# Holes of four partitions in both the loads and the scatters of five groups, and a reset instead of a drain, in a rank-and-scatter kernel

## The chip, the cores and the metric

The kernel runs on one core of a Trainium2 chip. The metric is the device time of one execution in microseconds (us). All executions quoted here count as fast ones. The kernel before takes 775.2 us (median of 4 executions beside the changed kernel, 775.0 to 775.73).

## The reference

Each row of 2,560 floats of `x` goes to the row of the output that its score's rank names, batch by batch:

```python
B, N, D = 8, 2048, 2560
order = np.argsort(scores, axis=1)
ranks = np.argsort(order, axis=1)
out[b_idx, ranks, :] = x          # 168 MB read, 168 MB written
```

The arithmetic is small (DVE counts, for each score, how many others of its batch are smaller). The work is to move 168 MB in and 168 MB out.

## The kernel before

A batch is cut into eight groups of 256 rows; in a group each of the 128 partitions holds two neighbouring rows of `x` (20,480 bytes). 58 groups go through eight buffers: Pool issues a load, and later two indirect scatters of 128 rows of 10,240 bytes. The first group of batches 0 to 5 takes another way: SP and ACT copy its rows one by one from DRAM to DRAM (the "row copies").

A transfer (DMA) is split over 16 DMA engines into packets: in the trace each of Pool's 204 loads and scatters shows as 128 packets, one per partition, and 16 that count up a semaphore; each row copy as 16 packets of 640 bytes and 16 of 4. A "hole" is four partitions of a group that its scatters leave out; their eight rows go by row copies instead. "The engine of 48-51" (or of 44-47) is short for the DMA engine that a hole at these partitions relieves. The trace names no engines, but it shows the relief: in the kernel before, the two scatters of group (5,4), with a hole at 48-51, take the part of one engine from 0.1 us behind the other late one to 2.3 us ahead of it. "Landing" is the moment at which a part of a transfer is reported done.

```python
DIRECT = range(6)            # batches whose group 0 goes by row copies
NBUF, LAG = 8, 4
THIN = {**{(b, 4): 48 for b in range(1, B)}, (7, 5): 44}   # the holes: (batch, group): first partition
HALVED = range(32)           # loads issued in two halves of 10,240 bytes per partition
# ... for a group in THIN, N is added to the ranks of four partitions: out of bounds, so not scattered
nc.gpsimd.indirect_dma_start(
    out=out_flat,
    out_offset=bass.IndirectOffsetOnAxis(ap=rank_i[:, col:col + 1], axis=0),
    in_=xb[k % NBUF][:, j * D:(j + 1) * D], in_offset=None, element_offset=b * N * D,
    **(dict(bounds_check=N - 1, oob_is_err=False) if (b, g) in THIN else {}),
).then_inc(s_scat[k % NBUF][j], 16)
# ... and the eight rows of a hole are row copies too (thin_rows)

for k, (b, g) in enumerate(BULK):                 # Pool's loop
    if k >= LAG and k + NBUF - LAG < len(BULK):
        scatters_done(pl, k - LAG)                # buffer free
        load_ahead(k + NBUF - LAG)
    pl.wait(*loaded[k])
    pl.after(dve, t_bulk[b, g])                   # ranks of this group
    for j in range(GROUPS[g][1]):
        scatter(k, j)
nc.gpsimd.drain()
for k in range(max(0, len(BULK) - NBUF), len(BULK)):
    scatters_done(sp, k)
```

## Time and profile before

| what | number | where |
|---|---|---|
| time | 775.2 us | executions |
| span of the profiled execution | 772.8 us | page |
| DVE, the busiest compute engine | 400.7 us busy | page, part 1 |
| moved by DMA | 320.15 MB, mean 414 GB/s | page, part 2 |
| last of the 16 parts of the last scatter lands | 770.56 us | semaphore records |
| from there to the end of the span | 2.24 us | the same |

The prediction shows the DMA rows. Two more views of the kernel before: First the page's part of the costliest groups: line, engine, operation, output and input, count; then busy us and mean ns; then the engine's idle time ahead of them and what ended most of it.

```profile
L424 POOL DMA_INDIRECT out_dram<-x,rank_i x116 | 113.4, 977 | 139.6 <-issue 35.0
L126 POOL DMA_DIRECT2D x<-in_x_dram x88 | 49.4, 565 | 436.9 <-DMA out_dram<-x,rank_i 418.5
```

Pool's own work is 113 + 49 us of 773; it stands idle 437 us ahead of its loads. It has room for dearer issues. Second, the page's list of DMA issues: output and input, queue, count and KB each:

```profile
x<-in_x_dram POOLq DMA_DIRECT2D x62, 1280.0 KB
x<-in_x_dram POOLq DMA_DIRECT2D x26, 2560.0 KB
out_dram<-in_x_dram ACTq DMA_DIRECT2D x800, 10.0 KB
out_dram<-in_x_dram SPq DMA_DIRECT2D x800, 10.0 KB
```

62 half loads and 26 whole ones by Pool, and 800 row copies on each of ACT and SP: 128 for each of six batches, and 32 for the holes.

### The profile page before, as it was taken

The numbers are of one execution on the slowest core, as the hardware profiler recorded it, in microseconds if no ns is written. First come the engines' busy times: TensorE is split into PE (matmuls) and PEld (weight loads), VectorE is DVE, ScalarE is ACT, GpSimd is POOL, SyncE is SP. The second block draws the span as 40 slices with busy tenths as digits, with TensorE's granted clock in tenths as the row PEclk, the third lists the DMA queues.
The fourth block names the chain that finished last, engine by engine and source line by source line (L and its number), as shares of the span: only waits on it lengthen the run. The fifth ranks groups of instructions, "written<-read, shape, count | busy, mean of one in ns | idle before, by whom it ended". The sixth has DMA issues, their size and how long they took to land.

```text
span 772.8 us, 8228 instructions
## 1 busy us (share of the span) xinstructions
PE 36.2 (5%) x172; PEld 30.4 (4%) x172; DVE 400.7 (52%) x828; ACT 0.0 (0%) x1; POOL 164.6 (21%) x213
## 2 busy tenths in 40 slices
PE   4000020020020020030000000000000000000000
PEld 3000010010010010030000000000000000000000
DVE  5999979979979979979999500000000000000000
ACT  0000000000000000000000000000000000000000
POOL 4114223222213131312112121212121212112100
PEclk8555555555555555565555555555555555555555
DMA  8999999999999999999999999999999999999996
GB/s 358 418 418 420 418 418 418 418 417 418 418 420 417 420 417 417 419 417 419 416 421 421 422 416 426 416 427 417 422 417 424 417 426 415 424 418 424 419 414 283
DMA packets 80898, 320.15 MB, mean 414 GB/s; under 512 B 28968, under 2 KB 54568, under 8 KB 54568
## 3 DMA queue, kind: packets, MB, share of 16 engines
q0 software_dynamic: 29376, 300.82, 91.7%
q1 hardware_dynamic: 25904, 10.93, 5.2%
q10 hardware_dynamic: 25600, 8.24, 4.3%
q14 instruction: 17, 0.14, 0.0%
q8 instruction: 1, 0.02, 0.0%
HBM read 168.49 MB, written 168.43 MB: 436 GB/s over the span
## 4 chain that ended last, share of the span: by engine, by line
DMA 63%; DVE 13%; another core or an unknown queue 9%; POOL 6%; issue 4%; PE 1%; POOLq 0%; SPq 0%
DMA out_dram<-x,rank_i 57%; DVE trash L239 12%; DMA x<-in_x_dram 6%; POOL out_dram L424 4%; POOL x L126 2%; PE ps_all L196 0%; DVE s_all L341 0%; DMA s_in<-in_scores_dram 0%; PE ps_col L175 0%; POOLq L448 0%; DVE rank_i L277 0%; DVE rank L271 0%; DVE rank L265 0%; PE ps_row L300 0%
## 5 line engine op out<-in xcount | busy, mean ns | idle before, releaser
L239 DVE TENSOR_SCALAR_CACHE_REDUCE trash<-s_all,s_col 128x1792 bf16<-128x1792 f32 (+7 forms) x240 | 315.2, 1348 | 4.6
L424 POOL DMA_INDIRECT out_dram<-x,rank_i x116 | 113.4, 977 | 139.6 <-issue 35.0
L126 POOL DMA_DIRECT2D x<-in_x_dram x88 | 49.4, 565 | 436.9 <-DMA out_dram<-x,rank_i 418.5
L239 DVE SCALAR_TENSOR_TENSOR trash<-s_all,s_col,mask 128x256 bf16<-128x256 f32 x128 | 61.6, 482 | 0.0
L196 PE MATMUL ps_all<-ident,s_col 128*128 128x128 f32 x128 | 28.1, 411 | 3.2 <-DVE s_all L341 2.8
L300 PE MATMUL ps_row<-ident,rank 128*1 128x128 f32 x28 | 8.3, 398 | 393.6 <-DVE rank_i L286 386.4
L196 PEld LDWEIGHTS ps_all<-ident,s_col 128*128 128x128 f32 x128 | 26.5, 222 | 4.2 <-DVE s_all L341 3.2
L341 DVE COPY s_all<-ps_all 128x512 f32<-128x512 f32 x32 | 20.2, 685 | 1.5 <-PE ps_all L196 1.1
L239 DVE DVE_READ_ACCUMULATOR trash<-s_all,s_col 128x1 f32 x240 | 19.9, 83 | 0.0
L300 PEld LDWEIGHTS ps_row<-ident,rank 128*1 128x1 f32 x28 | 2.0, 97 | 397.9 <-DVE rank_i L286 389.5
L311 DVE TENSOR_SCALAR thin_i<-ps_row 1x8 int32<-1x8 f32 x8 | 1.2, 154 | 19.0 <-PE ps_row L300 19.0
L239 DVE DVE_READ_ACCUMULATOR trash<-s_all,s_col,mask 128x1 f32 x128 | 10.7, 83 | 0.0
L326 DVE TENSOR_SCALAR rows_i<-ps_row 1x256 int32<-1x256 f32 x6 | 2.5, 412 | 4.1 <-PE ps_row L300 4.1
L183 DVE COPY s_col<-ps_col 128x128 f32<-128x128 f32 x1 | 0.3, 293 | 4.7 <-PE ps_col L175 4.7
L175 PE MATMUL ps_col<-ident,s_in 8*128 8x8 f32 x16 | 2.1, 262 | 3.9 <-DMA s_in<-in_scores_dram 3.9
L286 DVE TENSOR_SCALAR rank_i<-rank,hole 128x2 int32<-128x2 f32 x8 | 2.1, 262 | 0.3
L175 PEld LDWEIGHTS ps_col<-ident,s_in 8*128 8x128 f32 x16 | 2.0, 211 | 3.9 <-DMA s_in<-in_scores_dram 3.9
L277 DVE CAST rank_i<-rank 128x16 int32<-128x16 f32 (+3 forms) x11 | 1.9, 173 | 0.4
L271 DVE TENSOR_TENSOR rank<-rank,acc 128x16 f32<-128x16 f32 (+3 forms) x11 | 1.9, 171 | 0.4
L265 DVE TENSOR_TENSOR rank<-acc,acc 128x16 f32<-128x16 f32 (+3 forms) x11 | 1.9, 170 | 0.4
L156 POOL TENSOR_SCALAR_AFFINE_SELECT mask<-mask 128x256 f32<-128x256 f32 x2 | 0.8, 398 | 0.0
L168 DVE MEMSET acc<- 128x128 f32 x1 | 0.2, 165 | 1.1 <-SPq L102 1.1
(10 smaller groups left out, 1.8 us busy)
## 6 DMA issues: line engine op xcount, KB each, us to landing
x<-in_x_dram POOLq DMA_DIRECT2D x62, 1280.0 KB
x<-in_x_dram POOLq DMA_DIRECT2D x26, 2560.0 KB
out_dram<-in_x_dram ACTq DMA_DIRECT2D x800, 10.0 KB
out_dram<-in_x_dram SPq DMA_DIRECT2D x800, 10.0 KB
x<-in_x_dram SPq DMA_DIRECT2D x2, 1280.0 KB, 9.1
out_dram<-x,rank_i POOLq DMA_INDIRECT x116, 49.0
s_in<-in_scores_dram SPq DMA_DIRECT2D x1, 64.0 KB
```

The source lines that it names most:

```text
L126: line.eng.dma_start(out=xb[k % NBUF][:, part], in_=rows[:, part]).then_inc(sem, 16)
L175: nc.tensor.transpose(out=ps_col[:, B * c:B * (c + 1)], in_=s_in[:, r + j:r + m * P:m], identity=ident[:B, :B],)
L196: nc.tensor.transpose(out=ps_all[:, P * c:P * (c + 1)], in_=s_col[:, c, b:b + 1].to_broadcast([P, P]), identity=ident[:],)
L239: do(out=trash[i][:, :P * (hi_c - lo_c)], in0=s_all[:, P * lo_c:P * hi_c], accum_out=acc[i][:, col:col + 1], **how,)
L265: nc.vector.tensor_tensor(out=rank[:, cols], in0=acc[0][:, cols], in1=acc[1][:, cols], op=OP.add)
L271: nc.vector.tensor_tensor(out=rank[:, cols], in0=rank[:, cols], in1=acc[2][:, cols], op=OP.add)
L277: nc.vector.tensor_copy(out=rank_i[:, cols], in_=rank[:, cols])
L286: nc.vector.tensor_scalar(out=rank_i[:, cols], in0=rank[:, cols], scalar1=hole[:, i:i + 1], scalar2=None, op0=OP.add,)
L300: nc.tensor.transpose(out=ps_row[:1, P * j:P * (j + 1)], in_=rank[:, col:col + 1], identity=ident[:],)
L326: nc.vector.tensor_scalar(out=rows_i[b][:].rearrange("o (p j) -> o p j", p=P), in0=ps_row[:1, :WIDE].rearrange("o (j p) -> o p j", p=P), s ...
L341: nc.vector.tensor_copy(out=s_all[:, 512 * q:512 * (q + 1)], in_=ps_all[:, 512 * q:512 * (q + 1)],)
L424: nc.gpsimd.indirect_dma_start(out=out_flat, out_offset=bass.IndirectOffsetOnAxis(ap=rank_i[:, col:col + 1], axis=0), in_=xb[k % NBUF][:, ...
```

## The change

Its intent: a hole in the load as well as in the scatter should relieve the DMA engine of those partitions twice (by the packets' measured times, the four holes at 48-51 by 24.0 us, where seven in the scatters alone gave 21.0), so that five holes do the work of eight; fewer rows then go by row copies; and the end no longer waits for a drain. To leave a hole in a load, the load becomes a gather: an indirect load that takes its rows from a list (`thin_row`), in which the rows of the hole are out of bounds. The kernel before ends Pool's work with `drain()`, the changed one with `dma_reset()`: begun after the last landing, the drain took 2.60 us (run 5) and the reset 0.30 us.

```diff
-    THIN = {**{(b, 4): 48 for b in range(1, B)}, (7, 5): 44}
+    THIN = {**{(b, 4): 48 for b in range(1, B, 2)}, (7, 5): 44}
+    THIN_LOADS = [k for k in THIN if k[0]]
-    HALVED = range(32)
+    HALVED = range(34)
 ...
+            if (b, g) in THIN_LOADS:
+                i = HOLES.index(THIN[b, g])
+                line.after(dve, t_thin[0])
+                nc.gpsimd.indirect_dma_start(
+                    out=xb[k % NBUF][:, :m * D], out_offset=None,
+                    in_=x.rearrange("b (q j) d -> (b q) (j d)", j=m),
+                    in_offset=bass.IndirectOffsetOnAxis(ap=thin_row[:, i:i + 1], axis=0),
+                    element_offset=(b * N + r) * D, bounds_check=P - 1, oob_is_err=False,
+                ).then_inc(sem, 16)
 ...   # thin_row: two DVE operations after batch 0; partition number, plus N in the hole
-        nc.gpsimd.drain()
         for k in range(max(0, len(BULK) - NBUF), len(BULK)):
-            scatters_done(sp, k)
+            scatters_done(pl, k)
+        nc.gpsimd.dma_reset()
```

(`FLAT = ()` and the function `copies` only reshape the row-copy loop; they change none of its instructions.)

More of the change, by code (lines that the diff above doesn't have):

```diff
@@ L63 @@
     G = 16
-    THIN = {**{(b, 4): 48 for b in range(1, B)}, (7, 5): 44}
+    FLAT = ()
+    THIN = {**{(b, 4): 48 for b in range(1, B, 2)}, (7, 5): 44}
     HOLES = sorted(set(THIN.values()))
-    HALVED = range(32)
+    THIN_LOADS = [k for k in THIN if k[0]]
+    HALVED = range(34)
     STEPS = [(0, 1), (1, 2), (2, 4), (4, 8)]
@@ L90 @@
     hole = pool.tile([P, len(HOLES)], F32, name="hole")
+    below = pool.tile([P, 1], F32, name="below")
+    thin_row = pool.tile([P, len(HOLES)], I32, name="thin_row")
     thin_i = {k: pool.tile([1, 4 * MMAX], I32, name=f"thin_i{k[0]}_{k[1]}") for k in THIN}
@@ L118 @@
         n_load = [0] * NBUF
+        t_thin = []
         def load(line, k, sem):
@@ L122, in load @@
             r, m = GROUPS[g]
+            if (b, g) in THIN_LOADS:
+                i = HOLES.index(THIN[b, g])
+                line.after(dve, t_thin[0])
+                nc.gpsimd.indirect_dma_start(
+                    out=xb[k % NBUF][:, :m * D],
+                    out_offset=None,
+                    in_=x.rearrange("b (q j) d -> (b q) (j d)", j=m),
+                    in_offset=bass.IndirectOffsetOnAxis(ap=thin_row[:, i:i + 1], axis=0),
+                    element_offset=(b * N + r) * D,
+                    bounds_check=P - 1,
+                    oob_is_err=False,
+                ).then_inc(sem, 16)
+                n_load[k % NBUF] += 1
+                return
             rows = x[b, r:r + P * m, :].rearrange("(p j) d -> p (j d)", j=m)
@@ L334, in rows_to_bytes, with thin_rows_of_loads @@
             )
+        def thin_rows_of_loads():
+            dve.did(
+                nc.vector.tensor_reduce(
+                    out=below[:], in_=mask[:, MMAX, :], axis=mybir.AxisListType.X, op=OP.add
+                )
+            )
+            dve.after(dve, dve.n)
+            t_thin.append(
+                dve.did(
+                    nc.vector.tensor_scalar(
+                        out=thin_row[:],
+                        in0=hole[:],
+                        scalar1=below[:],
+                        scalar2=None,
+                        op0=OP.add,
+                    )
+                )
+            )
         for b in range(B):
@@ L358 @@
                         thin_to_bytes(b, g)
+            if b == 0:
+                thin_rows_of_loads()
         n_rows = {sp: 0, act: 0}
@@ L391, with copies @@
                 half = WIDE // 2
-                with line.eng.Fori(0, half // G) as q:
+                def copies(q):
+                    first = b * N + GROUPS[0][0] + half * h
                     _, at = nc.values_load_multi_w_load_instructions(
@@ L402 @@
                     for i in range(G):
-                        row = b * N + GROUPS[0][0] + half * h + i
                         line.eng.dma_start(
                             out=out_bytes[bass.ds(at[i], ROW)],
-                            in_=x_bytes[bass.ds(q * (G * ROW) + row * ROW, ROW)],
+                            in_=x_bytes[bass.ds(q * (G * ROW) + (first + i) * ROW, ROW)],
                         ).then_inc(s_rows[line], 16)
+                if b in FLAT:
+                    for q in range(half // G):
+                        copies(q)
+                else:
+                    with line.eng.Fori(0, half // G) as q:
+                        copies(q)
                 n_rows[line] += half
```

## The prediction

> **What bounds the kernel now.** I looked first at the page's rows of busy tenths. Every compute engine is light: DVE, the busiest, works 400.7 of 772.8 us and ends shortly after 400. The row that is full from start to end is DMA's.
>
> ```profile
> DMA  8999999999999999999999999999999999999996
> GB/s 358 418 418 420 418 418 418 418 417 418 418 420 417 420 417 417 419 417 419 416 421 421 422 416 426 416 427 417 422 417 424 417 426 415 424 418 424 419 414 283
> ...
> q0 software_dynamic: 29376, 300.82, 91.7%
> q1 hardware_dynamic: 25904, 10.93, 5.2%
> q10 hardware_dynamic: 25600, 8.24, 4.3%
> ```
>
> The tenths stay at 9 in slices 2 to 39; only the first slice (start) and the last (283 GB/s against some 418) are lower. The three queues' shares add up to over 100% of 16 engines' time. So I read the packet records one by one: from 2 us on, a packet starts as the one before it on its DMA engine ends, and in the whole run I find only some 20 holes of 0.3 us. On its engine a packet of 10,240 bytes takes 381 ns, one of 20,480 bytes 757, one of 640 bytes 28 and one of 4 bytes (a semaphore) 6. The time is therefore each DMA engine's own sum of packets, and the end is that of the slowest engine of the 16. What sets it is which packets that engine has, not a wait.
>
> The view of the waits seems to say otherwise:
>
> ```profile
> POOL x L126 <- DMA out_dram<-x,rank_i: 418.5, 45, 11.2
> POOL out_dram L424 <- issue: 35.0, 108, 1.5
> POOL out_dram L424 <- DMA x<-in_x_dram: 34.6, 4, 10.8
> POOL out_dram L424 <- DVE rank_i L286: 25.7, 1, 25.7
> ```
>
> Pool waits 418.5 us for scatters before it may reload a buffer. But while it waits [...] (a scatter lands 49.0 us after its issue), so these waits starve nothing, and neither does the one of 25.7 us for DVE's ranks: the load issued before it still landed 7 us after it ended.
>
> Then I looked at the end. The semaphore records give the landing of each of the 16 parts of a DMA. For the last scatter twelve parts land 4.6 to 3.6 us before the last one, two at 3.0 and 2.5 us before it, one 1.2 us before it, and the last at 770.56 us. Two engines are thus late, by some 4 and 3 us against the twelve. For SP's queue the waits show what follows:
>
> ```profile
> SPq L28 <- DMA out_dram<-x,rank_i: 33.1, 8, 12.5
> SPq L392 <- DVE rows_i L326: 15.6, 1, 15.6
> SPq L102 <- POOLq L102: 0.9, 1, 0.9
> ```
>
> SP has its last scatter at 770.58 us and is then held 0.9 us by Pool. The record of the drain explains it:
>
> ```profile
> engine op xcount: duration ns min/median/max, first and last start us, forms
> L448 POOLq DRAIN  x1: 32437/32437/32437, 739.5 to 739.5; - x1
> ```
>
> It ends at 739.48 + 32.44 = 771.92 us, 1.36 us after the last landing. The closing barrier follows, and the span ends at 772.8: 2.24 us lie between the last landing and the end.
>
> [...] The trace names no engines[...]: in the scatters of group (5,4), whose hole is 48-51, the engine that trailed the other late one by 0.1 us is ahead of it by 2.3 us afterwards; 8 packets of 381 ns are 3.05 us.[...]
>
> What a skipped row costs can be counted: 88 loads and 116 scatters of Pool are 204 DMAs, and 204 * (128 + 16) = 29376, the packets of q0, although 64 rows were skipped; in the records 64 packets of 4 bytes are there beyond the 204 * 16 semaphores. A skipped row is a 4-byte packet of some 6 ns.
>
> Why the late engines are late: the 10,240-byte packets that took more than 386 ns come, after 430 us, in runs of some 14, some 430 ns apart, every 13 us. That is one engine, in its two scatters (then the only transfers with that size), at some 20 to 27 ns extra a packet. The holes at 48-51 pay for that; the change pays more with fewer holes.
>
> **The change part by part.**
>
> (1) Row copies. 8 holes of 8 rows were 64 rows; 5 holes are 40. 24 row copies fall away, each 28 + 6 = 34 ns on every engine: -0.82 us on all 16.
>
> (2) Engine of 48-51. Before: 7 groups, 56 scatter packets skipped, 56 * (381 - 6) = 21.0 us. After: 4 groups, 32 scatter packets, 12.0 us, and now also 4 * 4 load packets of 20,480 bytes, 16 * (757 - 6) = 12.0 us; together 24.0. It gains 3.0 us. It processes 24 more scatter packets, at some 20 ns extra each: 0.5 us back. Net -2.5.
>
> (3) Engine of 44-47. Before: 8 * 375 ns = 3.0 us. After: the same and 4 * 751 ns = 3.0 more. Net -3.0.
>
> (4) Halved loads. Groups (1,4) and (3,4), number 10 and 24 in the order, were halved and are now gathers; the limit of 34 halves numbers 32 and 33 instead. So 62 half loads remain, and 21 whole loads and 5 gathers stand for 26 whole ones: no net packets.
>
> (5) Pool's issue. An indirect issue takes 977 ns on Pool and a direct one 565; five gathers, two of which replace two issues each, cost about a microsecond of an engine that sits idle before its loads for 437 us. Nothing. The wait for DVE's row list comes at load 10, where the ranks of batch 0 have been waited for already by scatter 3. Two more small DVE operations (some 0.4 us) delay batch 1 by less than the 7 us of slack seen above. Nothing.
>
> (6) The end. The drain goes; Pool waits for the last scatters itself and then resets. The wait would end some 0.03 us after the landing, as SP's did. If the reset is as short as the other drains of Pool at the end (34 to 72 ns), Pool reaches the barrier some 0.15 us after the landing rather than 1.40, and 1.2 us are gained; since nothing shows the reset's cost, I take 1.1.
>
> Sum at the end of the DMA. The last packets of the engines lie at 770.1 and 769.0 (the late two), 767.7 and 767.2 (the two between) and 765.6 to 766.6 (twelve). I cannot tell which of the late two is which. After: 770.1 - 0.8 - 2.5 or 3.0 = 766.3 to 766.8; 769.0 becomes 765.2 to 765.7; the two between, which no hole touches, 766.9 and 766.4; the twelve 764.8 to 765.8. So the last engine is now an untouched one at 766.9, and the DMA ends 3.2 us sooner. With (6): 3.2 + 1.1 = 4.3 us, 775.31 - 4.3 = **771.0 us**, 0.6% less.
>
> **The rivals.** First, nothing but the end: the gathers might be dealt to the engines by another rule than loads, or a skipped load row might still move. For it: no gather is in the trace of before.[...] The engines of the holes would then be relieved by less than before (12 instead of 21 us) and the first would end some 9 us later, less 0.8: with the end's gain, about 782 us. Second, balance turned over: an engine that lags up to 6 us in the batches without hole could let buffers come free later.[...] If it does, 1 to 2 us of the gain go: 772 to 773. Third, the reset costs as much as the drain or more, since it takes the place of the drain on the path: then only the 3.2 us remain, or less, 772 to 773. Fourth, the load's own extra cost also goes with the skipped packets, or the two between shift too: 770.
>
> **Range and chances.** The sum of 4.3 has parts of different certainty: 0.8 and the packets' arithmetic are firm, the floor by the untouched engines is read from the trace; the reset is open by about a microsecond. 769.6 to 773.0 should hold it 8 times in 10. 2% is 15.5 us, out of reach on the fast side: faster 0.01, within 2% 0.97, slower 0.02 (the first rival and worse).
>
> **What would show it.** Bytes of q0 300.82 - 0.41 + 0.25 = 300.66 MB in 29376 packets as before; 25648 packets on q1 and 25088 on q10. The rows of issues: 62 half loads, 21 whole, 5 indirect loads. The sixteen parts of the last scatter should land within some 2.5 us instead of 4.6, the last near 767.4 us, and the span should end about 1.1 us after it, with no drain of 32 us. If the spread stays at 4 us or more, steps (2) and (3) are wrong; if the span ends 2 us or more after the last landing, step (6) is; if DMA's tenths fall below 9 in the middle, the second rival holds.

A last landing 3.2 us sooner and 1.1 us of the end come to 4.3 us, and 775.31 - 4.3 = 771.0 us. Terms (2) and (3) put the four partitions of a hole on one engine, and 48-51 and 44-47 on two different ones. What the traces show of it: in the kernel before, after 430 us, 12 to 15 slow packets (10,240 bytes in over 389 ns) stand together in the two scatters of a group, and only 7, 5 and 5 in the holed groups (4,4), (5,4) and (6,4). In the changed kernel two parts land late, by 6.5 and 5.4 us at 688 us against the median of the first twelve; after the load of (7,4), with its hole at 48-51, one of the two is down to 3.9 us (694 us), and after that of (7,5), with its hole at 44-47, the other to 3.0 and then 2.6 (708 and 721 us). Against the first rival: a scatter is indirect too, and its hole did relieve an engine, by 2.4 us in group (5,4). Against the second, and for the harmless waits, stands that a scatter lands 49.0 us after its issue, while the longest wait of Pool for a buffer is 11.2 us. The last row copies landed at 764.1 us (SP) and 762.1 us (ACT).

## The result, and the profile after

The changed kernel took 771.38 us (median of 4, 771.06 to 771.9) beside 775.2 us before: 3.8 us less. The ratio is 0.995, with an interval of 0.9933 to 0.9967. All ratios here are the mean time of one kernel's fast runs over that of the other's of the same rounds, so not quite the ratio of the quoted medians. Predicted were 771.0 us and a range of 769.6 to 773.0: right. (The two profiled executions took 774.87 and 771.55 us, 3.3 us apart, with spans of 772.8 and 769.8; the 0.4 us by which the spans differ less lie outside them, and the traces do not show what they are.)

The page after, rows of busy tenths, rates and queues (packets, MB, share of 16 engines):

```profile
DMA  8999999999999999999999999999999999999997
GB/s 356 420 419 418 418 421 417 417 419 419 418 417 417 416 419 417 419 419 418 417 418 418 425 417 423 417 422 419 422 417 423 419 420 422 419 425 416 426 411 332
...
q0 software_dynamic: 29376, 300.66, 92.0%
q1 hardware_dynamic: 25648, 10.85, 5.2%
q10 hardware_dynamic: 25088, 8.08, 4.2%
```

The bytes and packets of q0 and the packets of q1 and q10 are the predicted ones to the digit. DMA is full to the end as before; the last slice moves 332 instead of 283 GB/s, which fits the better balance. Pool's waits after:

```profile
POOL x L149 <- DMA out_dram<-x,rank_i: 391.3, 43, 11.1
...
POOL x L135 <- DMA out_dram<-x,rank_i: 40.3, 4, 10.3
...
POOL out_dram L476 <- DVE thin_row L369: 19.3, 1, 19.3
```

391.3 + 40.3 = 431.6 us of waits for a buffer stand for 418.5 before; four of them now come ahead of a gather (L135). The 19.3 us for `thin_row` is no new wait: before, the same 19.3 us stood under another DVE line, and the tie now falls on the last DVE instruction of that time. The gathers among the costliest groups, and the queue's issues:

```profile
L135 POOL DMA_INDIRECT x<-in_x_dram,thin_row x5 | 5.2, 1031 | 43.9 <-DMA out_dram<-x,rank_i 40.3
```

```profile
x<-in_x_dram POOLq DMA_DIRECT2D x62, 1280.0 KB
x<-in_x_dram POOLq DMA_DIRECT2D x21, 2560.0 KB
out_dram<-in_x_dram SPq DMA_DIRECT2D x792, 10.0 KB
out_dram<-in_x_dram ACTq DMA_DIRECT2D x784, 10.0 KB
...
x<-in_x_dram,thin_row POOLq DMA_INDIRECT x5
```

A gather costs Pool 1,031 ns, 466 more than a direct load's 565, on an engine with 430 us to spare. Row copies fell from 1,600 to 1,576.

The end, in the waits of SP's queue and in the record of the reset:

```profile
SPq L109 <- DMA out_dram<-in_x_dram: 27.7, 1, 27.7
...
SPq L109 <- POOLq L109: 11.1, 1, 11.1
```

```profile
L503 POOLq DRAIN  x1: 296/296/296, 768.7 to 768.7; - x1
```

SP has no scatter to wait for any more: it sees its last row copy land and waits 11.1 us for Pool, which sees the last scatter at 768.57 us, resets in 0.30 us (the reset is recorded as a drain) and closes. The span ends 1.28 us after the last landing, before 2.24 us. Of the span's 3.0 us (772.8 - 769.8), 2.0 are a sooner last landing (770.56 to 768.57) and 1.0 is the shorter end. The 16 parts of the last scatter lie within 3.6 us, before 4.6.

One measure is used from here on. The **lag** of a DMA engine is how much later its part of a scatter lands than the median of the first twelve of the 16 parts. In the last scatter of the kernel before the two largest lags are 4.2 and 2.9 us, in the changed one 2.8 and 1.8.

### The profile page after: what moved, and what is told of

The parts are those of the page before. It is cut to its first block, busy times and chain, and to the rows that moved or that the text cites. A ratio compares the mean times of both kernels' runs of the same rounds, so it can differ in the third digit from the quotient of the medians.

```text
span 769.8 us, 8160 instructions
## 1 busy us (share of the span) xinstructions
PE 33.4 (4%) x166; PEld 29.2 (4%) x166; DVE 400.1 (52%) x824; ACT 0.0 (0%) x1; POOL 167.1 (22%) x213
## 4 chain that ended last, share of the span: by engine, by line
DMA 63%; DVE 13%; another core or an unknown queue 10%; POOL 6%; issue 4%; PE 1%; POOLq 0%; SPq 0%
DMA out_dram<-x,rank_i 57%; DVE trash L262 12%; DMA x<-in_x_dram 6%; POOL out_dram L476 4%; POOL x L149 2%; DVE s_all L384 0%; POOL x L135 0%; PE ps_all L219 0%; DMA s_in<-in_scores_dram 0%; PE ps_col L198 0%; DVE rank_i L300 0%; DVE rank L294 0%; DVE rank L288 0%; PE ps_row L323 0%
## 5 line engine op out<-in xcount | busy, mean ns | idle before, releaser
L149 POOL DMA_DIRECT2D x<-in_x_dram x83 | 46.7, 564 | 393.3 <-DMA out_dram<-x,rank_i 391.3
L323 PE MATMUL ps_row<-ident,rank 128*1 128x128 f32 x22 | 5.9, 365 | 388.7 <-DVE rank_i L309 281.5
L135 POOL DMA_INDIRECT x<-in_x_dram,thin_row x5 | 5.2, 1031 | 43.9 <-DMA out_dram<-x,rank_i 40.3
```

The source lines that it names most:

```text
L135: nc.gpsimd.indirect_dma_start(out=xb[k % NBUF][:, :m * D], out_offset=None, in_=x.rearrange("b (q j) d -> (b q) (j d)", j=m), in_offset=b ...
L149: line.eng.dma_start(out=xb[k % NBUF][:, part], in_=rows[:, part]).then_inc(sem, 16)
L323: nc.tensor.transpose(out=ps_row[:1, P * j:P * (j + 1)], in_=rank[:, col:col + 1], identity=ident[:],)
```

## The experiments

Theory: each DMA engine has a fixed sum of packets; the one of partitions 48-51 is far later than the others, and holes take packets from it; reset against drain is worth 1 us. The main rivals: the gathers relieve nothing and only the 24 row copies count; the late engine is held or bounded by the buffers; the end gives nothing. Three sessions: the first four runs shared one chip and its runs of the kernel before (775.1 us, 11 executions), the last eight another (774.95 us, 9 to 10). All outputs were correct.

### 1. The end alone

The kernel before with the lines of the end alone changed:

```diff
-        nc.gpsimd.drain()
         for k in range(max(0, len(BULK) - NBUF), len(BULK)):
-            scatters_done(sp, k)
+            scatters_done(pl, k)
+        nc.gpsimd.dma_reset()
```

> The kernel before with the new end alone (Pool waits for the last scatters, then resets; no drain). Theory: in the trace the part after the last landing falls from 2.24 us to about 1.28 us, as in the changed kernel, and nothing else moves: 775.2 - 1.0 = 774.2 us. Rival: the old drain's tail is mostly time in which the trace's last landing is not the last write, so the reset only moves the wait elsewhere: 775.0 to 775.4 us.

Measured: 774.94 us (773.96 to 777.32), ratio 1.000 (0.9987 to 1.0012). A miss for the theory: nothing gained. The trace says why. Its waits of SP's queue:

```profile
SPq L102 <- DMA out_dram<-in_x_dram: 27.0, 1, 27.0
...
SPq L102 <- ACTq L102: 0.2, 1, 0.2
```

No line has SP wait for Pool: SP waits for ACT. The last landing of all is a row copy of ACT, at 772.13 us, after the last scatter at 771.56. In the kernel before the row copies had ended at 764 us. Nothing of the row copies was edited. When they end is not fixed from execution to execution (SP's at 757.5 us in the changed kernel's first trace and at 764.6 in its second, run 9). The last scatter too landed 1.0 us later than in the kernel before (771.56 against 770.56), which alone would have used up the gain: 771.56 + 1.28 = 772.84, where the span before was 772.8. So this run does not show what the end is worth. Runs 11 and 12 below test it.

### 2. The change without its end

The changed kernel with the old four lines of the end.

> The changed kernel with the old end (drain, SP waits). Theory: the two parts add up: 771.4 + 1.0 = 772.4 us, with the last landing near 768.6 us as in the changed kernel. Rival (the ends interact with the holes): 771.4 or 773 and more.

Measured: 771.6 us (770.92 to 772.06), ratio 0.9952 (0.9939 to 0.9965). In time it is 0.2 us from the changed kernel (another session). In the trace the last scatter lands at 767.19 us and the drain ends at 768.51, 1.32 us later, as before (1.36). But a row copy of SP lands only at 768.96: here too a row copy is last, and the drain is hidden behind it. The expectation, 772.4 us, was 0.8 too high: the last scatter landed 1.4 us sooner than the 768.6 that it assumed. In time, nearly all of the gain of the change came without its end; the two medians are of two sessions, so 0.2 us between them is no measurement of the end.

### 3. Holes in the scatters alone

```diff
-    THIN_LOADS = [k for k in THIN if k[0]]
+    THIN_LOADS = []
```

(and the two DVE operations for `thin_row` left out)

> The changed kernel with its five holes in the scatters alone; the loads of these groups are direct and whole rows. Theory: the engine of 48-51 has 16 load packets of 757 ns more, 12.0 us, that of 44-47 3.0 us more. If the engine of 48-51 is the last one of the changed kernel (last part at 768.57 us) the last landing comes at 780.6 us, if it is the second (767.58) at 779.6: time 782.4 to 783.4 us, with one part landing alone some 12 us after the others. Rival: the gathers relieve little, the gain was the 24 fewer row copies: 771 to 774 us.

Measured: 780.37 us (780.21 to 780.41), ratio 1.0067. The rival falls: without the holes in the loads the five holes are worse than the old eight. One part lands alone, with a lag of 11.1 us. The row of DMA shows what a single late engine looks like, a last slice of which the others fill only the first third:

```profile
DMA  8999999999999999999999999999999999999993
```

The expectation was 2 to 3 us too high: the 16 load packets gave less than 12.0 us.

### 4. No holes at all

```diff
-    THIN = {**{(b, 4): 48 for b in range(1, B, 2)}, (7, 5): 44}
-    HOLES = sorted(set(THIN.values()))
+    THIN = {}
+    HOLES = [44, 48]        # only so that the unused tile has columns
```

> No holes, no thin row copies, new end: shows each engine's own lateness. Theory: the engine of 48-51 loses its relief of 24.0 us (and processes 32 more scatter packets at some 20 ns extra, 0.6 us), that of 44-47 6.0 us, all 16 gain 40 row copies of 34 ns, 1.4 us. Last landing at 767.6 or 768.6 + 24.6 - 1.4 = 790.8 to 791.8 us, time 793.6 to 794.6 us, one part some 18 us after the second, the second some 5 to 6 us after the third. Rival (lateness is not fixed work of an engine but bounded by the buffers, so that a late engine holds up the others and the spread stays near 6 us): the DMA tenths fall below 9 in the middle and the time lies below 790 us with a spread of 6 to 10 us.

Measured: 789.8 us (789.71 to 790.29), ratio 1.019. The lateness is seen naked:

```profile
DMA  8999999999999999999999999999999999999980
GB/s 359 418 418 420 418 418 418 419 418 419 417 417 417 419 419 419 418 419 415 420 417 420 425 416 423 419 421 419 426 416 424 417 425 418 422 422 423 423 349 24
```

In the last slice one engine of 16 works (24 of some 420 GB/s). In the last scatter its lag is 21.9 us; the second engine's is 3.5, the next two have 0.9, the others under 0.3. The expected time, 793.6 to 794.6 us, was some 4 us too high: the holes had been counted at their full size. DMA stays at 9 until the others run out, so the buffers do not hold them up: the rival falls here too (the time is below 790 us as it said, but the lag is 21.9 us and not 6 to 10). The lag grows until some 710 us (4 us at 150, 10 at 290, 15 at 400, 18 at 510, 22 at 670, 23.4 at 708 us) and then no more.

Now the holes can be weighed by the lag of this engine:

| kernel | packets skipped on it | their time by the prediction's arithmetic | lag at the end | lag taken away |
|---|---|---|---|---|
| no_holes | 0 | 0 | 21.9 us | |
| scatter_holes | 32 of 10,240 bytes | 12.0 us | 11.1 | 10.8 |
| before | 56 of 10,240 | 21.0 | 4.2 | 17.7 |
| changed | 32 of 10,240, 16 of 20,480 | 24.0 | 2.8 (1.7 in a second trace) | 19.1 (20.2) |

(For the last two it is assumed that the last engine is the same one; if it is another, this one was relieved of more. Each lag in the table is of one trace. Four traces have the eight holes of before: before, end_only, end_rows and rows_only, with largest lags of 3.8 to 5.3 us and a mean of 4.3. Four have the changed kernel's holes: its own two, old_end and wait_drain, with 1.6 to 2.8 and a mean of 2.0.) Holes give 80 to 90% of what the packets alone would. Where the rest goes is partly seen: in the kernel before, slow packets beside the holed scatters of groups (4,4) to (7,4) carry 200 to 320 ns more than usual (at 453.2, 454.9, 545.4, 547.1, 650.7, 652.4, 749.1 and 751.2 us). In the changed kernel the other holed engine's lag falls in one holed scatter from 2.56 to 1.35 us: 1.2, not the 1.5 of four packets. A transfer with a hole thus gives some 0.3 us back. In the first 400 us no such packets stand out, so this is not the whole account, and why they are slow is not shown.

### 5. A drain after the waits

The changed kernel with `drain()` in place of `dma_reset()`; Pool still waits for the scatters first.

> The changed kernel with a plain drain in place of the reset; Pool still waits for its last scatters first. Tells the waits from the reset. Theory A (the drain [...]is slow by itself): the drain, begun at the last landing, still takes over 0.6 us where the reset took 0.30, and the tail after the last landing is 1.6 to 2.3 us. Theory B (the drain is short once all has landed): under 0.3 us, tail 1.3 us or less. The time is 771.2 to 771.8 us either way, since two earlier runs showed that the end is worth 0.2 us of time or less when a row copy can be the last transfer.

Measured: 772.84 us (772.53 to 773.38), ratio 0.997 (0.9957 to 0.9984). In the trace the drain begins when all has landed and takes

```profile
L503 POOLq DRAIN  x1: 2602/2602/2602, 767.8 to 767.8; - x1
```

2.60 us against 0.30 for the reset. Theory A holds in that the drain is slow with nothing left in flight; the tail is longer than it said (3.59 us, not 1.6 to 2.3). In the kernel before the drain began at 739.5 us and only 1.36 us of it came after the last landing; that it did the rest beside the transfers is an inference. The expected time, 771.2 to 771.8, was missed: here the scatters are last (767.69 us, row copies 764.7), so the tail counts in full. Against the changed kernel on the same chip (run 9, 772.06 us) it is 0.8 us slower.

### 6 and 7. One more hole on either engine

```diff
+    (6, 4): 48   added to THIN, in the scatters alone     # more_48
+    (6, 5): 44   added to THIN, in the scatters alone     # more_44
```

> The changed kernel with one more hole at 48-51, in the scatters of group (6,4) alone; 8 more row copies. Theory: the last part in the changed kernel is the engine of 48-51, 2.8 us behind the median of the twelve; eight packets fewer take 3.0 us from it, less 0.3 us for each holed transfer; 8 row copies add 0.3 us to all. Its lag falls to 0.2 to 0.8 us, the spread of the last scatter to some 2.5 us, the next engine sets the end at about 767.8 us, and the time falls 0.5 to 1.0 us, to 770.4 to 770.9. Rival (another engine is the last one): the time rises by the 0.3 us.

> The changed kernel with one more hole at 44-47, in the scatters of group (6,5) alone. Theory: the engine of 44-47 is already among the twelve at the end, so nothing is gained and the 8 row copies cost 0.3 us: 771.4 to 771.9. Rival (it is the last one): 770.4 to 770.9 us. Seen in time, its lag of 5.4 us falls by some 2.6 us at the scatters of (6,5), near 660 us, and not by 3.0, if a holed transfer gives 0.2 us back.

Measured: more_48 772.56 us (771.79 to 772.69), more_44 772.08 us (770.83 to 774.45); ratios 0.9964 and 0.9968. For more_48 the largest lag is 1.8 us, the next 1.2, and the last scatter lands at 767.54 us, near the expected 767.8. But the changed kernel's own second trace, on the same chip, has 1.7 us and 767.35 without the extra hole (run 9), so a gain from it is not shown. The time was missed: a row copy of SP lands at 769.13 us, 1.6 us after the last scatter, and closes the kernel. For more_44 the lag of the engine with the hole at 44-47 falls as expected (5.3 us at 654 us, 2.9 at 677, of which not all readings can be kept apart), and there is no gain (772.08 us, a little above the expected 771.4 to 771.9); its executions scatter over 3.6 us, and row copies (767.91 us) and scatters (767.74) end together.

### 8. Gathers without holes

The offset that put the hole's rows out of bounds is multiplied by zero, so that the gathers leave nothing out:

```diff
-    in0=hole[:], scalar1=below[:], scalar2=None, op0=OP.add,
+    in0=hole[:], scalar1=0.0, scalar2=below[:], op0=OP.mult, op1=OP.add,
```

> The changed kernel whose five gathers fetch all 128 rows; the scatters keep their holes. Against scatter_holes (780.4 us) it shows what a gather costs as such. Theory: nothing, 780.2 to 780.8 us, one part 11 us behind the others. Rival (gathers are dealt to the engines differently, or are slower): over 781.5 us, or a spread that is not that of one late engine.

Measured: 780.42 us (779.97 to 781.53), ratio 1.0071; largest lag 11.2 us. Against scatter_holes, 780.37 and 11.1: a gather as such costs nothing here. The holes in the loads are worth what lies between this and the changed kernel: 8.4 us on the same chip (772.06, run 9), 9.0 against the first session's 771.4.

### 9. The changed kernel again

> The changed kernel once more, as the yardstick on the chip of the next three: 771.1 to 771.9 us, 3.8 us under the kernel before.

Measured: 772.06 us, just above the expected range, six executions from 770.34 to 775.39, ratio 0.9965 (0.9946 to 0.9984). The profiled one (770.34) has its last landing at 767.35 us, a spread of 3.0 us and a largest lag of 1.7; the end after it is again 1.28 us. On this chip the change is worth 2.9 us (774.95 to 772.06), not 3.8. The median is 0.7 us above the first session's and one execution of six is 3.3 us above the median. The slow executions have no trace, so what they lost cannot be read.

### 10, 11 and 12. Row copies sooner

Each of these has `HALVED = range(38)`; for more_48 it stood at 34, for end_only and for the kernel before at 32.

> more_48 with 38 instead of 34 loads halved. In more_48 the row copies of SP ended last (769.1 us, 1.6 us after the last scatter). Theory: [...] the row copies end near 755 us or before, the scatters near 767.7, the tail is 1.3 us, and the time is 770.4 to 771.0, the fastest of all. Rival (the row copies' pace is set by the issue of SP and ACT[...]): they still end within 5 us of the scatters, and the time stays at 772 to 773.

> end_only with 38 instead of 32 loads halved. In end_only the row copies ended last (772.1 us) and the end gained only 0.2 us. Theory: with the row copies 20 us sooner the end shows its worth: tail 1.28 us, 774.0 to 774.4 us and a narrower spread of the runs than end_only's 3.4 us. Rival (the reset itself makes the next execution's transfers end a microsecond later): 774.8 to 775.4 us, the runs as scattered as before.

> The kernel before with 38 instead of 32 loads halved, nothing else: the control of end_rows. Theory: 48 more packets on each engine at some 5 ns more, 0.2 us; the scatters were last already, so 775.2 to 775.5 us, and end_rows lies 0.9 to 1.2 us under it. Rival: end_rows and this agree within 0.4 us.

Measured: rows_only 774.88 us (774.66 to 775.23), end_rows 773.77 us (773.06 to 774.04), more_48_rows 771.55 us (771.38 to 775.38); ratios to the kernel before 0.9995, 0.9981 and 0.9964. The first two lie 0.2 to 0.3 us below their expected ranges, the third 0.55 above: in its trace a row copy is last again (767.9 us, the last scatter 767.6).

end_rows and rows_only differ in the end alone, and in both traces the row copies end early (at 756 and 762 us at the latest). The end is then worth 774.88 - 773.77 = 1.1 us, and the runs of end_rows spread over 1.0 us instead of 3.4. In the traces the tail after the last scatter is 2.49 us in rows_only and 1.65 in end_rows (not the 1.28 of the other traces with the reset): 0.84 us shorter. Their lines of SP's waits show the two cases:

```profile
SPq L102 <- POOLq L102: 14.2, 1, 14.2
```

in end_rows (SP done early, Pool's reset closes), and

```profile
SPq L28 <- DMA out_dram<-x,rank_i: 36.3, 8, 16.4
...
SPq L102 <- POOLq L102: 1.2, 1, 1.2
```

in rows_only (SP sees the last scatter and then waits 1.2 us for the drain). So the end gains about 1 us when the scatters are last. That it gains nothing when a row copy is last fits end_only and old_end, but was not tested by itself.

That more halved loads bring the row copies sooner did not hold as a rule. From end_only to end_rows they ended 15.5 (SP) and 19 us (ACT) sooner, as expected; from the kernel before to rows_only 2 us (SP) and 9 us (ACT); from more_48 to more_48_rows SP's 1.2 us sooner and ACT's 4.7 us later, where some 14 us sooner were expected of both. That was the estimate, on an account of the row copies' pace that no trace shows. What sets their pace stays open.

The traces show one thing more. The late engine's slow packets (10,240 bytes in 389 to 459 ns, where the others take 385) are there while row copies run beside them and stop when these do. Counted from 1 us after the start of the last packet of a row copy, such packets are 2 of 430 in end_rows (last row copy 756 us), of which one engine of 16 would have had some 27, 0 of 199 in rows_only (762) and 0 of 98 in the kernel before (764). In end_only, whose row copies last until 772 us, they are still 8 of 51 after 765 us. In no_holes none of the 62 packets after 765 us is slow: there the late engine soon works alone, and the row copies ended at 747; between 757 and 764 us, however, several engines at once have slow ones there. The largest lag at the end goes the same way in the four traces with eight holes: 3.8 us with the last row copy at 756, 3.9 at 762, 4.2 at 764, 5.3 at 772. So the lateness does not seem to be a fixed property of this engine's packets, but something that happens to them beside row copies. No run without row copies tests that, and why it is this engine stays open.

No version is shown to beat the changed kernel: more_48_rows has a median 0.5 us lower on the same chip, but the ratios are 0.9964 and 0.9965.

## Why the prediction was right

**What bounds the kernel**: right. The DMA engines are full (tenths of 9 in slices 2 to 39), and the end is that of the slowest. no_holes shows it plainest: its last scatter ends with one engine, 21.9 us late. One reading was wrong without consequence: the "some 20 holes of 0.3 us" are no idle time. Taking each packet's engine from the times, 21 gaps of over 0.2 us appear among the packets of the loads, scatters and row copies, and 17 of them are filled by the 17 packets of q14 ("instruction" in the profile), of some 309 ns each.

**(1) Row copies**, -0.82 us on all engines: about right. The median of the first twelve parts of the last scatter came 0.67 us sooner (766.40 to 765.73 us).

**(2) The engine of 48-51**, net -2.5 us beside the others: right in direction. The largest lag fell from 4.2 us to 2.8 in one trace (-1.3) and to 1.7 in the other (-2.4); the means over four traces each, given under run 4, fell by 2.2 (two of the four with eight holes have 38 loads halved). The term that was mis-sized is the skipped packet: "a skipped row is a 4-byte packet of some 6 ns" leaves out what a holed transfer gives back. Against no_holes, 21.0 us of packets took away 17.7 and 24.0 took away 19.1 or 20.2. Most of the error was in both kernels, so their difference suffered little: of the 3.0 us of packets 1.3 or 2.4 came, where the prediction had allowed for 2.5. The sign of it was in the prediction's own reading: at group (5,4) the holed engine went from 0.1 us behind the other late one to 2.3 us ahead, which is 2.4 us of the 3.05 that it set beside it; the difference was passed over.

**(3) The engine of 44-47**, -3.0 us: nearly right. In the changed kernel its lag fell from 5.4 to 2.6 us with the hole in the load of (7,5), and by another 1.2 us in the first of its two holed scatters.

**The floor at 766.9 us by an untouched engine**, with the last landing near 767.4 us and the parts within some 2.5 us, did not come in the first trace: the last part landed at 768.57 us, and the spread was 3.6 us. In the other three traces with these holes (run 9, old_end, wait_drain) the last landing was at 767.35, 767.19 and 767.69 us, with spreads of 3.0, 2.2 and 3.6. Their mean with the first is 767.7, and that of the four traces with eight holes 770.8: 3.1 us sooner, where 3.2 had been predicted. Whether the last engine is then an untouched one was not seen.

**(4) and (5)**: right. 62 half loads, 21 whole ones and 5 gathers; gathers at 1.03 us of an idle engine; gather_all shows that they cost nothing else.

**(6) The end**, 1.1 us: right in the trace (0.96; the reset took 0.30 us, not the 0.03 to 0.07 of a late drain) and in the pair end_rows and rows_only (1.1 us of time, 0.84 in their traces).

**The rivals.** The first (gathers relieve nothing) is what scatter_holes and gather_all imitate: 780.4 us where the prediction had said about 782. The second (buffers) is excluded by no_holes: even a lag of 22 us starved nobody until the end. The third (a dear reset) is excluded by the reset's 0.30 us. The fourth (770 us, more relief than counted) did not come: the holes gave less.

**What the prediction did not see** is that the row copies are a second stream that can end last. It read 764 us from one trace and took them as safe. In the other traces the last of them landed at 747 to 772 us. The expectations for end_only, more_48 and more_48_rows missed with a row copy as the last landing, and it may be why the same kernel had a median of 771.4 us in one session and 772.1 in another; that last step is argued, not shown. How near 771.0 the first session's 771.4 came is therefore partly luck; both medians lie in the predicted range.

## What to carry to other kernels

When all DMA engines are full, compare their ends, not the waits: the sixteen landings of the last transfer tell which engine is late and by how much, and taking a few rows from it can be worth more than bytes saved on all (here 8.4 to 9.0 us for the holes in five loads, 0.7 us for 24 row copies less). A kernel with all its holes removed shows the lags at once, and should be run before the holes are tuned; here the lag of 21.9 us was known only after the prediction. And when two streams end within a few microseconds of each other, a gain on one may be hidden in executions in which the other is last (the new end showed no gain in run 1, where a row copy landed last, and 1.1 us in runs 11 and 12), so a change of 1 us has to be tested with the other stream moved out of the way.

## What else the traces show

- The ends: 2.60 us for the drain with all landed (204 transfers, wait_drain), 1.32 to 1.60 us left over in three traces in which it began some 30 us before the last landing (before, old_end, rows_only), 0.30 us for the reset.
- The engine that a hole at partitions 48-51 relieves was the slow one, with a lag of 21.9 us of 787 without holes; no other engine lagged by more than 3.5 us in that scatter. Its extra time is in its scatters, whose packets of 10,240 bytes took on average some 20 to 25 ns more than 385 after 430 us (the records overlap by 4 ns, so 385 here is the prediction's 381); near the end, where it can be told, this stopped with the row copies.
- A skipped row of an indirect DMA stays in the queue as a packet of 4 bytes (64 of them in the kernel before, 60 in the changed one), and a transfer with a hole gave some 0.3 us of the saved time back.
- The trace of the kernel before shows 17 packets of 8,192 bytes on q14, named "instruction"; each takes some 309 ns of an engine, and in 16 of the 17 cases a packet that begins as it ends takes 87 to 610 ns longer (at 93.2 us one of q14, at 93.5 us a packet with 346 ns more). Which engines they fall on was not found.
